# Earlier first half of a final norm, and attention heads that turn in two events, in a one-layer macaron block

## The chip, the cores and the metric

The program runs on one core of a Trainium2 chip. The core has a matrix engine (TensorE, PE in the rows, with its weight loads as PEld), a vector engine (VectorE, DVE), an activation engine (ScalarE, ACT), GpSimd (POOL) and an engine that mostly issues transfers (SyncE, SP). Each of them works through its own instructions in order and waits on semaphores for the others. The metric is the device time of one execution in microseconds. Profile times are microseconds from the first instruction of one profiled execution.

## The reference

For 512 tokens of 1024 features, everything in 32-bit floats, the program computes

```python
x = x + 0.5 * swiglu(rmsnorm(x, ffn1_norm), w_gate1, w_up1, w_down1)      # 2816 wide
x = x + token_mixer(rmsnorm(x, mix_norm), w_in, w_out, ...)
x = x + 0.5 * swiglu(rmsnorm(x, ffn2_norm), w_gate2, w_up2, w_down2)
return rmsnorm(x, final_norm)
```

The mixer has 4 differential heads (two 64-wide query/key maps and one 128-wide value each) and 8 dilated heads. A differential head is

```python
p = softmax(q @ k.T * scale + bias)          # causal, for both maps
a = p[:, :, 0] - lam * p[:, :, 1]
out = rmsnorm(a @ v, subln_gain) * (1 - lam0)
```

so a query block i of 128 tokens needs the key blocks 0 to i: 1, 2, 3 and 4 blocks of 128x128 for the four query blocks, 10 in all. `rmsnorm(x, g)` is `x * rsqrt(mean(x*x) + 1e-6) * g`.

## The kernel before

The residual x lies transposed in SBUF: eight tiles x[0..7] of 128 features by 512 tokens. Weights and activations are split in a high part of a faster number format and a low rest (fp32r in the rows), and each product is three matrix products (`mm3`, lines 123 to 125). Where an operand isn't split (turns, values, sums for a norm), the product runs in plain 32-bit floats: a value product of 128x128 is then two instructions on TensorE, a turn (a transposition against the identity) one.

**Mixer.** TensorE's stream is a list of chunks: per unit "q0, v0, q1, v1, q2, q3, q4, v2, q5, q6, v3, q7" eight chunks. A q chunk has 6 products of 512 columns, a v chunk 12 of 256 columns. `put(t, rank, f)` hangs work on chunk t: before the chunk's own products, by rank, come the events of rank under 10. TensorE, VectorE and ScalarE get exactly this order (manual schedule), so all three queues are set by the table of chunk numbers at the end of `attention`. A head u that starts at chunk s (12, 29, 45 and 53 for the differential heads 0 to 3) does:

- `score(m, i)` (TensorE L1058 and L1059, VectorE L1061, ScalarE L1064) for map m of query block i at chunk s + 2i + m. The scores lie in PSUM tiles "s", of which there are two: a score waits until VectorE has read the one before the last.
- `combine(i)` (VectorE L1068, L1071, L1075) at s + 2i + 3: it makes the weighted difference of the two maps.
- `turn(0, i)` at s + 5 + 2i: i + 1 transpositions (L1127) into a PSUM tile "t" (two of these) and a ScalarE copy to SBUF (L1130). `values(0, i)` two chunks later: i + 1 products with the values (L1139), so values(i) and turn(i+1) stand at the same chunk. Five chunks have such an event.
- from chunk e = s + 14: `squares` (ScalarE), `mean` and the root's steps (VectorE), `scale` (VectorE L1162), `finish` (four transpositions L1168 into a "t" tile, and ScalarE), `finish_low` (VectorE L1182), at e, e+1, e+2, e+3, e+4, e+6, e+7.

Dilated heads (4 to 7) have their own functions (`turn_part`, L1094 and L1105, two "t" tiles per event), with one SBUF tile "tx".

**The last stage.** The second FFN ends with products for half the tokens at a time: for feature tiles 6 and 7 first the left 256 tokens (`plb`), then the right ones (`prb`); each is 6 steps k of three products. While the right ones run, `last` lets the left half's final norm begin: sums of squares on TensorE (L1375), root and reciprocal with a correction step (`final_rstd`), a diagonal from it (L1400), a product that spreads it over all partitions (L1405), then VectorE multiplies (L1412) and SyncE writes out. After the last right product, `final_end` does the same for the right half by transpositions (L1423), scaling (L1432, L1434) and five output transfers (L1437).

Of the kernel before, what the change touches and what calls it, by code (L numbers as in the profile page):

```python
# [14 lines left out]
F32 = mybir.dt.float32  # L15
# [3 lines left out]
ALU = mybir.AluOpType  # L19
AX = mybir.AxisListType  # L20

P = 128
S = 512
D = 1024
FF = 2816
KD = D // P
JF = FF // P
HD = 64
NQ = S // P
EPS = 1e-6  # L30
# [13 lines left out]
PLAIN = 6  # L44
# [10 lines left out]
HS = S // 2  # L55
# [4 lines left out]
OFF = [0, 128, 384, 768]  # L60
# [3 lines left out]
def tile_macaron(ctx: ExitStack, tc, xs, xT, wf, wgu1, wst1, wd1, wdg1, wqk, wv, wo, wgu2, wst2, wd2,  # L64
                 wdg2, lams, relb, onehot, addc, out):
    nc = tc.nc
    V, A, G, T = nc.vector, nc.scalar, nc.gpsimd, nc.tensor
# [4 lines left out]
    tp = ctx.enter_context(tc.tile_pool(name="tp", bufs=2))  # L72
    wp = ctx.enter_context(tc.tile_pool(name="wp", bufs=3))
    sp = ctx.enter_context(tc.tile_pool(name="sp", bufs=4))
# [6 lines left out]
    def mm_bank(nm):  # L81
        return pp.tile([P, S], F32, tag="mm", name=nm, bufs=4)
# [651 lines left out]
    with tc.manual_schedule(engines={mybir.EngineType.DVE, mybir.EngineType.Activation}):  # L734
        for t in range(4):
            raw = wp.tile([P, 1024], F32, tag="raw", name=f"raw_f{t}")
            h, l = w_place()
            for kk in range(2):
                k = 2 * t + kk
# [134 lines left out]
    def put(t, rank, f, *a):  # L874
        at.setdefault(t, []).append((rank, f, a))
# [163 lines left out]
    def attention(u, s):  # L1039
# [80 lines left out]
                             skip_group_check=True)  # L1120
                n += w

        def turn(m, i):
            w = (i + 1) * P
            pt = pp.tile([P, S], F32, tag="t", name=f"pt{u}{m}{i}", bufs=2)
            for k in range(i + 1):
                T.transpose(pt[:, k * P:(k + 1) * P],  # L1127
                            st["pr"][m][:, OFF[i] + k * P:OFF[i] + (k + 1) * P], ident[:])
            ptb = tp.tile([P, S], F32, tag="ptb", name=f"ptb{u}{m}{i}", bufs=2)
            A.copy(ptb[:, :w], pt[:, :w])  # L1130
            st["ptb", m, i] = ptb

        def values(m, i):
            if "po" not in st:
                st["po"] = mm_bank(f"po{u}")
                st["po3"] = st["po"][:].rearrange("p (i d) -> p i d", i=NQ)
            fo = (u % 4) * P
            for k in range(i + 1):
                T.matmul(st["po3"][:, i, :], st["ptb", m, i][:, k * P:(k + 1) * P],  # L1139
                         vt[0, k][:, fo:fo + P], start=k == 0, stop=k == i)  # L1140

        def squares():
            ob_ = tp.tile([P, S], F32, tag="ob", name=f"ob{u}")
# [51 lines left out]
            put(s + step * i + (1 if quick else 3 if diff or i < 3 else 2),  # L1195
                5 if diff or quick or i != 2 else 6.5, combine, i)
        if diff:
            tv = max(s + 5, v_end[u])
            for i in range(NQ):
                put(tv + 2 * i, 2, turn, 0, i)  # L1200
                put(tv + 2 * i + 2, 1, values, 0, i)
            e = tv + 9
            put(e, 7, squares)
            put(e + 1, 7, mean)
            for j in range(4):
                put(e + 2 + j // 2, 8, lambda j=j: st["rs"][j]())
            put(e + 4, 7, scale)
            put(e + 6, 3, finish)
            put(e + 7, 8, finish_low)
        elif quick:  # L1210

            for j, part in enumerate((((0, 0, 3),), ((1, 1, 3), (2, 2, 3)),
                                      tuple((k, 3, 4) for k in range(NQ)))):
                for m in range(2):
                    put(s + 4 + j, 2, turn_part, m, part)
                put(s + 5 + j, 1, values_part, part)
            put(s + 7, 3, finish)
            put(s + 7, 4, finish_low)
        else:
            tv = max(s + 9, v_end[u])  # L1220
            parts = ((0, 0, 4),), ((1, 1, 4),), ((2, 2, 4), (3, 3, 4))
            for j, part in enumerate(parts):
                for m in range(2):
                    put(tv + j, 2, turn_part, m, part)
                put(tv + 4, 1, values_part, part)
            put(tv + 5, 3, finish)
            put(tv + 5, 8, finish_low)
# [110 lines left out]
    def last(t, m, o, k, put):  # L1338


        hh = int(o == "r")
        c = half(hh)
        if k == PLAIN:
            q = fin.setdefault("sq", {})
            if m not in q:
                q[m] = slot(8 + m - (KD - 2), f"sql{m}")
            put(t, A.activation, q[m][:, c], x[m][:, c], AF.Square)
            put(t, weighted, m, hh)
            if m == KD - 2 and o == "l":
                put(t, lambda: V.tensor_tensor(sq[:, c], sq[:, c], q[m][:, c], op=ALU.add))  # L1350
            if (o, m) == ("r", KD - 1):
                put(t, final_end)
        elif (o, m, k) == ("l", KD - 2, 0):
            A.activation(root[:], eps[:], AF.Sqrt)
        elif (o, m, k) == ("r", KD - 2, PLAIN - 4):
            final_sums(0, sq, True, False)
        elif (o, m, k) == ("r", KD - 2, PLAIN - 3):
            final_sums(0, fin["sq"][KD - 1], False, True)
            final_rstd(0)
            spread_parts()  # L1360
        elif (o, m, k) == ("r", KD - 1, PLAIN - 4):
            final_spread()
            final_left(0)
            final_left(1)
            final_left(2, 0, 1)

    def final_sums(hh, src, first, end):

# [9 lines left out]
    def final_rstd(hh):  # L1378
        ps, n = fin["ps", hh], NQ // 2
        y = sp.tile([P, n], F32, tag="ly", name=f"ly{hh}")  # L1380
        t = sp.tile([P, n], F32, tag="lt", name=f"lt{hh}")
        w = sp.tile([P, n], F32, tag="lw", name=f"lw{hh}")
        A.activation(y[:], ps[:, :n], AF.Sqrt, bias=eps[:])
        V.tensor_scalar(w[:], ps[:, :n], EPS, -0.5, op0=ALU.add, op1=ALU.mult)
        V.reciprocal(y[:], y[:])

        for i in range(n):
            c = slice(i, i + 1)
            V.scalar_tensor_tensor(t[:, c], y[:, c], w[:, c], y[:, c], op0=ALU.mult, op1=ALU.mult)
        V.scalar_tensor_tensor(y[:], t[:], 1.5, y[:], op0=ALU.add, op1=ALU.mult)  # L1390
        fin["y", hh] = y

# [15 lines left out]
    def final_left(g2, a=0, b=2):  # L1408
        n = b - a
        r = fin["pb"][:, :HS].rearrange("p (o q) -> p o q", o=1).to_broadcast([P, n, HS])  # L1410
        y2 = fin[0, g2][:, a * HS:b * HS].rearrange("p (m q) -> p m q", m=n)
        V.tensor_tensor(y2, y2, r, op=ALU.mult)  # L1412
        m = 2 * g2 + a
        nc.sync.dma_start(
            out[0, m * P * HS:(m + n) * P * HS].rearrange("(m p q) -> p m q", p=P, q=HS), y2)
# [23 lines left out]
            fin[b, g4, "o"][:, c0:c1])  # L1439

    def final_end():
        final_left(2, 1, 2)
        final_left(3)
        final_sums(1, sq, True, False)
        final_sums(1, fin["sq"][KD - 2], False, False)
        for m in (0, 1):
            for b in range(2):
                turned(m, b)
        final_sums(1, fin["sq"][KD - 1], False, True)
        for m in range(2, KD):  # L1450
            for b in range(2):
                turned(m, b)
        final_rstd(1)
        final_right(0, 0, V, 0, HS)
        right_out(0, 0, 0, HS)
        final_right(1, 0, A)
        final_right(0, 0, V, HS, S)
        right_out(1, 0)
        right_out(0, 0, HS, S)
        final_right(0, 1, V)  # L1460
        final_right(1, 1, A)
        right_out(0, 1)
        right_out(1, 1)
# [105 lines left out]
```

## Time and profile before

| | |
|---|---|
| three runs | 931.29, 931.54, 931.55 us; median 931.54 |
| the profiled execution | 932.39 us; from first to last instruction 930.6 us |
| TensorE busy | 922.9 us (99%), granted clock 0.999 of full |
| VectorE, ScalarE, GpSimd busy | 727.9 (78%), 543.5 (58%), 98.3 us (11%) |
| transfers | 136.71 MB, 147 GB/s mean |
| the mixer's chunks | about 345 to 552 us |
| last right-half product to the end | about 921.0 to 930.6 us |

The profiled execution took 0.85 us more than the median, of which its span is 930.6 and 1.79 lie around it. A matrix instruction's duration overlaps with the next one's, so what it costs is read from the distance of two starts. "Busy" TensorE can also hold a short wait, which then shows as a longer distance and duration, not as idle time.

### The profile page before, as it was taken

The numbers are of one execution on the slowest core, as the hardware profiler recorded it, in microseconds if no ns is written. First come the engines' busy times: TensorE is split into PE (matmuls) and PEld (weight loads), VectorE is DVE, ScalarE is ACT, GpSimd is POOL, SyncE is SP. The second block draws the span as 40 slices with busy tenths as digits, with TensorE's granted clock in tenths as the row PEclk, the third lists the DMA queues.
The fourth block names the chain that finished last, engine by engine and source line by source line (L and its number), as shares of the span: only waits on it lengthen the run. The fifth ranks groups of instructions, "written<-read, shape, count | busy, mean of one in ns | idle before, by whom it ended". The sixth has DMA issues, their size and how long they took to land.

```text
span 930.6 us, 17116 instructions
## 1 busy us (share of the span) xinstructions
PE 922.9 (99%) x6402; PEld 854.7 (92%) x6402; DVE 727.9 (78%) x1504; ACT 543.5 (58%) x1122; POOL 98.3 (11%) x117
## 2 busy tenths in 40 slices
PE   9999999999999999999999999999999999999997
PEld 8888999999999999988979778889999999999997
DVE  7797887677888897668876556797888777888784
ACT  7454665355665575656766664455666455665573
POOL 0001100112202100000000003110120012111000
PEclk9999999999999999999999999999999999999999
DMA  7446646578757562434343213464774678875542
GB/s 260 121 144 154 158 122 177 138 182 210 201 131 207 138 176 94 132 97 129 97 136 92 68 48 133 114 173 102 183 189 120 162 199 193 209 178 153 136 126 91
DMA packets 59876, 136.71 MB, mean 147 GB/s; under 512 B 6848, under 2 KB 8128, under 8 KB 59792
## 3 DMA queue, kind: packets, MB, share of 16 engines
q1 hardware_dynamic: 45792, 110.14, 36.8%
q0 software_dynamic: 14000, 25.47, 17.6%
q8 instruction: 50, 0.82, 0.4%
q14 instruction: 34, 0.28, 0.1%
HBM read 130.30 MB, written 2.14 MB: 142 GB/s over the span
## 4 chain that ended last, share of the span: by engine, by line
PE 97%; DVE 2%; DMA 0%; issue 0%; ACT 0%; DVEq 0%; SPq 0%
PE pv L935 2%; PE pv L933 2%; PE pv L934 2%; PE pq L123 2%; PE pwo L123 2%; PE pq L124 2%; PE pq L125 2%; PE pk L125 2%; PE pk L123 2%; PE pk L124 2%; PE pwo L124 2%; PE pwo L125 2%; PE pua L125 2%; PE pua L124 2%; PE pua L123 2%; PE pda L124 1%
## 5 line engine op out<-in xcount | busy, mean ns | idle before, releaser
L1064 ACT ACTIVATE pr<-pr,mx 128x128 f32<-128x128 f32 (+3 forms) x64 | 36.1, 564 | 34.3 <-DVE mx L1061 34.0
L1061 DVE CUSTOM_DVE_ANT_0 pr<-sc,strip 128x128 f32<-128x128 f32 (+3 forms) x64 | 30.7, 488 | 22.4 <-PE sc L1059 22.0
L391 ACT CAST w<-s2b 128x512 fp32r<-128x512 f32 x50 | 31.1, 621 | 17.1 <-DVE s2b L373 14.8
L395 DVE TENSOR_TENSOR w<-s2b,w 128x512 fp32r<-128x512 f32 x50 | 34.3, 686 | 7.3 <-ACT w L391 7.3
L391 ACT CAST w<-s2a 128x512 fp32r<-128x512 f32 x46 | 28.6, 622 | 17.5 <-DVE s2a L373 14.6
L395 DVE TENSOR_TENSOR w<-s2a,w 128x512 fp32r<-128x512 f32 x46 | 31.5, 686 | 6.6 <-ACT w L391 6.6
L150 POOL TENSOR_TENSOR sq<-sq,sqt 128x512 f32<-128x512 f32 x7 | 10.9, 1564 | 240.2 <-ACT sqt L149 240.1
L933 PE MATMUL pv<-w,xh 128*128 128x256 f32 x128 | 36.2, 283 | 0.0
L935 PE MATMUL pv<-w,xh 128*128 128x256 f32 x128 | 36.2, 283 | 0.0
L934 PE MATMUL pv<-w,xl 128*128 128x256 f32 x128 | 36.2, 282 | 0.0
L123 PE MATMUL pq<-xh,w 128*128 128x512 f32 x64 | 26.3, 410 | 0.0
L123 PE MATMUL pwo<-mh,w 128*128 128x512 f32 x64 | 25.5, 399 | 0.0
L124 PE MATMUL pq<-xl,w 128*128 128x512 f32 x64 | 25.1, 393 | 0.0
L125 PE MATMUL pq<-xh,w 128*128 128x512 f32 x64 | 25.0, 391 | 0.0
L125 PE MATMUL pk<-xh,w 128*128 128x512 f32 x64 | 25.0, 391 | 0.0
L123 PE MATMUL pk<-xh,w 128*128 128x512 f32 x64 | 25.0, 391 | 0.0
L124 PE MATMUL pk<-xl,w 128*128 128x512 f32 x64 | 25.0, 391 | 0.0
L124 PE MATMUL pwo<-ml,w 128*128 128x512 f32 x64 | 25.0, 390 | 0.0
L125 PE MATMUL pwo<-mh,w 128*128 128x512 f32 x64 | 24.9, 390 | 0.0
L934 PEld LDWEIGHTS pv<-w,xl 128*128 128x128 f32 x128 | 24.4, 191 | 0.3
L933 PEld LDWEIGHTS pv<-w,xh 128*128 128x128 f32 x128 | 24.4, 191 | 0.2
L935 PEld LDWEIGHTS pv<-w,xh 128*128 128x128 f32 x128 | 24.5, 191 | 0.0
(709 smaller groups left out, 3997.9 us busy)
## 6 DMA issues: line engine op xcount, KB each, us to landing
raw_qk<-wqk_dram SPq DMA_DIRECT2D x16, 512.0 KB, 3.4
raw0bg<-wst_dram SPq DMA_DIRECT2D x9, 512.0 KB, 4.8
raw_gua<-wgu_dram SPq DMA_DIRECT2D x8, 512.0 KB, 3.5
raw0ag<-wst_dram SPq DMA_DIRECT2D x8, 512.0 KB, 4.7
raw0ad<-wdg_dram SPq DMA_DIRECT2D x8, 512.0 KB, 4.7
strip<-bias_rows SPq DMA_DIRECT2D x16, 256.0 KB, 3.7
raw_v<-wv_dram SPq DMA_DIRECT2D x8, 512.0 KB, 3.3
raw_wo<-wo_dram SPq DMA_DIRECT2D x8, 512.0 KB, 3.3
```

The source lines that it names most:

```text
L123: T.matmul(po, wh, mh, start=first, stop=False, skip_group_check=on)
L124: T.matmul(po, wh, ml, start=False, stop=False, skip_group_check=on)
L125: T.matmul(po, wl, mh, start=False, stop=last, skip_group_check=on)
L150: G.tensor_tensor(sq[:], sq[:], t[:], op=ALU.add)
L391: A.copy(made[t][0], source(t))
L395: V.tensor_tensor(l, source(t), h.bitcast(F32), op=ALU.subtract)
L933: T.matmul(po, xh[k][:, xs], wh[:, o:o + 256], start=k == 0, stop=False)
L934: T.matmul(po, xl[k][:, xs], wh[:, o:o + 256], start=False, stop=False)
L935: T.matmul(po, xh[k][:, xs], wl[:, o:o + 256], start=False, stop=k == KD - 1)
L1061: V.tensor_tensor_reduce(out=pi, in0=ps[:, :w], in1=st["b"][m][:, w - 1::-1], op0=ALU.add, op1=ALU.min, scale=1.0, scalar=3.0e38, accum_ou ...
L1064: A.activation(pi, pi, AF.Exp, scale=-1.0, bias=st["mx"][:, m, i:i + 1], accum_out=st["ls"][:, m, i:i + 1])
```

## The change

Differential heads: `turn` takes tuples of query blocks, each tuple shares one PSUM tile "t" and one ScalarE copy, and the copies go to the "tx" tile. Blocks 0 and 2 (1 + 3 transpositions) share a tile, block 1 has its own, both at chunk s + 8; block 3 at s + 10. All ten value products run at s + 12 (or at the end of the v unit, if that is later), and e comes one chunk earlier.

Final norm: both sums of the left half are made at the same step (k = 2 of the right product of tile 6), the spread product and the first multiplications come after k = 1 instead of k = 2 of tile 7, the multiplication of feature tiles 4 and 5 is no longer cut in two, and `final_rstd` has other operations.

```diff
+        def turn(tiles):
+            if "tx" not in st:
+                st["tx"] = tp.tile([P, 12 * HS], F32, tag="tx", name=f"ptx{u}", bufs=1)
+            for own in tiles:
+                pt = pp.tile([P, S], F32, tag="t", name=f"pt{u}{own[0]}", bufs=2)
+                n, c0 = 0, st.get("used", 0)
+                for i in own:
+                    st["place", i] = c0 + n
+                    for k in range(i + 1):
+                        o = OFF[i] + k * P
+                        T.transpose(pt[:, n:n + P], st["pr"][0][:, o:o + P], ident[:])
+                        n += P
+                A.copy(st["tx"][:, c0:c0 + n], pt[:, :n])
+                st["used"] = c0 + n
+        def values():
...
+            for i in range(NQ):
+                for k in range(i + 1):
+                    o = st["place", i] + k * P
+                    T.matmul(st["po3"][:, i, :], st["tx"][:, o:o + P],
+                             vt[0, k][:, fo:fo + P], start=k == 0, stop=k == i)
...
         if diff:
-            tv = max(s + 5, v_end[u])
-            for i in range(NQ):
-                put(tv + 2 * i, 2, turn, 0, i)
-                put(tv + 2 * i + 2, 1, values, 0, i)
-            e = tv + 9
+            put(s + 8, 2, turn, ((0, 2), (1,)))
+            put(s + 10, 2, turn, ((3,),))
+            tv = max(s + 12, v_end[u])
+            put(tv, 1, values)
+            e = tv + 1
...
             final_sums(0, sq, True, False)
-        elif (o, m, k) == ("r", KD - 2, PLAIN - 3):
             final_sums(0, fin["sq"][KD - 1], False, True)
             final_rstd(0)
             spread_parts()
-        elif (o, m, k) == ("r", KD - 1, PLAIN - 4):
+        elif (o, m, k) == ("r", KD - 1, PLAIN - 5):
             final_spread()
             final_left(0)
             final_left(1)
-            final_left(2, 0, 1)
...
-        V.tensor_scalar(w[:], ps[:, :n], EPS, -0.5, op0=ALU.add, op1=ALU.mult)
         V.reciprocal(y[:], y[:])
-        for i in range(n):
-            c = slice(i, i + 1)
-            V.scalar_tensor_tensor(t[:, c], y[:, c], w[:, c], y[:, c], op0=ALU.mult, op1=ALU.mult)
+        V.scalar_tensor_tensor(t[:], y[:], -0.5, y[:], op0=ALU.mult, op1=ALU.mult)
+        V.scalar_tensor_tensor(t[:], ps[:, :n], EPS, t[:], op0=ALU.add, op1=ALU.mult)
...
     def final_end():
-        final_left(2, 1, 2)
+        final_left(2)
```

TensorE's queue where head 2 (chunks 51 to 53) is scored, before: `sc` is a score, `pt` a turn, `po` a value product, and the left-out rows are chunk products.

```order
L1058 MATMUL sc_5052<-k_4811,q_4809 128x512
L1059 MATMUL sc_5052<-l_4813,q_4809 128x512
...
L1139 MATMUL po_5063<-v_4247,ptb_5034 128x128
L1127 MATMUL pt_5065<-ident,pr_4864 128x128 x2
L1058 MATMUL sc_5073<-k_4812,q_4810 128x512
L1059 MATMUL sc_5073<-l_4814,q_4810 128x512
...
L1058 MATMUL sc_5087<-k_4960,q_4958 128x256
L1059 MATMUL sc_5087<-l_4962,q_4958 128x256
```

The same place in the changed kernel:

```order
L1058 MATMUL sc_5038<-k_4804,q_4802 128x512
L1059 MATMUL sc_5038<-l_4806,q_4802 128x512
...
L1058 MATMUL sc_5052<-k_4805,q_4803 128x512
L1059 MATMUL sc_5052<-l_4807,q_4803 128x512
...
L1134 MATMUL pt_5067<-ident,pr_4858 128x128 x4
L1134 MATMUL pt_5073<-ident,pr_4858 128x128 x2
L1058 MATMUL sc_5077<-k_4950,q_4948 128x256
L1059 MATMUL sc_5077<-l_4952,q_4948 128x256
```

No turn or value product stands any more between the scores of head 2; its first turn event, with the blocks 0, 2 and 1, stands right before head 3's first score, one chunk after head 2's last score.

TensorE's queue around `finish` of head 3 (`ot`, four transpositions), after the last turn event of dilated head 4 (`pt`), before and then in the changed kernel:

```order
L1094 MATMUL pt_5576<-ident,pr_5215 128x128 x3
L1094 MATMUL pt_5581<-ident,pr_5216 128x128 x3
L123 MATMUL pq_5590<-xh_78,w 128x512
...
L125 MATMUL pk_5591<-xh_78,w 128x512
L1168 MATMUL ot_5607<-ident,ob_5471 128x128 x4
```

```order
L1094 MATMUL pt_5556<-ident,pr_5204 128x128 x3
L1094 MATMUL pt_5561<-ident,pr_5205 128x128 x3
L1175 MATMUL ot_5568<-ident,ob_5438 128x128 x4
L123 MATMUL pq_5578<-xh_78,w 128x512
```

The chunk that stood between them is now behind: three tiles "t" are wanted in a row, of which there are two.

VectorE's queue at the end (the multiplications of the left half by `bcl`, and the last right product's sum into x[7], written `x_103<-prb`), before and then in the changed kernel:

```order
L1412 TENSOR_TENSOR y_10053<-y_10053,bcl 128x512
L1412 TENSOR_TENSOR y_10189<-y_10189,bcl 128x512
L1412 TENSOR_TENSOR y_10315<-y_10315,bcl 128x256
L432 SCALAR_TENSOR_TENSOR x_103<-prb_10509,x_103 128x256
L1412 TENSOR_TENSOR y_10315<-y_10315,bcl 128x256
L1412 TENSOR_TENSOR y_10442<-y_10442,bcl 128x512
```

```order
L1414 TENSOR_TENSOR y_10033<-y_10033,bcl 128x512
L1414 TENSOR_TENSOR y_10169<-y_10169,bcl 128x512
L432 SCALAR_TENSOR_TENSOR x_103<-prb_10487,x_103 128x256
L1414 TENSOR_TENSOR y_10295<-y_10295,bcl 128x512
L1414 TENSOR_TENSOR y_10422<-y_10422,bcl 128x512
```

One multiplication of 256 columns moved from ahead of the sum into x[7] to behind it, joined to its other half.

## Rows read from the trace of the kernel before

**Rows 1.** The page's line of busy times, with share of the span and instructions.

```profile
PE 922.9 (99%) x6402; PEld 854.7 (92%) x6402; DVE 727.9 (78%) x1504; ACT 543.5 (58%) x1122; POOL 98.3 (11%) x117
```

**Rows 2.** All waits of TensorE: total us, times, longest.

```profile
PE warm L725 <- POOL ones_d L719: 1.0, 1, 1.0
PE pga L770 <- ACT w L750: 0.2, 1, 0.2
```

**Rows 3.** Timeline of TensorE, an event of head 1: start, us, instruction, count.

```profile
415.01 0.83 PE L1139 MATMUL po<-v,ptb 128*128 128x128 f32 x6
415.68 0.60 PE L1127 MATMUL pt<-ident,pr 128*128 128x128 f32 x4
...
416.35 0.40 PE L124 MATMUL pq<-xl,w 128*128 128x512 f32 x1
```

**Rows 4.** Timeline of TensorE, scores of head 2 and the chunk between.

```profile
436.38 0.38 PE L1127 MATMUL pt<-ident,pr 128*128 128x128 f32 x2
436.75 0.50 PE L1058 MATMUL sc<-k,q 128*128 128x512 f32 x1
...
437.33 0.39 PE L123 MATMUL pq<-xh,w 128*128 128x512 f32 x1
...
438.70 0.32 PE L1058 MATMUL sc<-k,q 128*128 128x256 f32 x1
```

**Rows 5.** Timeline of VectorE, the same stretch.

```profile
436.14 0.55 DVE L1061 CUSTOM_DVE_ANT_0 pr<-sc,strip 128x384 f32<-128x384 f32 x1
...
436.61 0.75 DVE L1182 SCALAR_TENSOR_TENSOR ml<-ot,sub,mh 128x512 fp32r<-128x512 f32 x1
...
438.94 0.62 DVE L1075 SCALAR_TENSOR_TENSOR pr<-pr,cc,pr 128x384 f32<-128x384 f32 x1
```

**Rows 6.** Timeline of VectorE, combinations of heads 1 (two) and 3.

```profile
408.49 0.62 DVE L1075 SCALAR_TENSOR_TENSOR pr<-pr,cc,pr 128x384 f32<-128x384 f32 x1
...
412.18 0.75 DVE L1075 SCALAR_TENSOR_TENSOR pr<-pr,cc,pr 128x512 f32<-128x512 f32 x1
...
454.01 0.62 DVE L1075 SCALAR_TENSOR_TENSOR pr<-pr,cc,pr 128x384 f32<-128x384 f32 x1
```

**Rows 7.** Timeline of TensorE where chunks 37 and 61 begin (61 with a score).

```profile
410.13 0.39 PE L123 MATMUL pq<-xh,w 128*128 128x512 f32 x1
...
455.90 0.28 PE L1058 MATMUL sc<-k,q 128*128 128x256 f32 x1
```

**Rows 8.** Timeline of TensorE, the last turn event of head 4.

```profile
478.55 0.82 PE L1094 MATMUL pt<-ident,pr 128*128 128x128 f32 x6
```

**Rows 9.** Timeline of ScalarE, the copies of that event.

```profile
479.07 0.86 ACT L1105 COPY ptx<-pt 128x384 f32<-128x384 f32 x2 [1.18 <-PE pt L1094]
```

**Rows 10.** ScalarE's copies by shape: count, total us, mean ns, idle before.

```profile
L1105 ACT COPY ptx<-pt 128x384 f32<-128x384 f32 x12 | 5.2, 484 | 3.7 <-PE pt L1094 3.6
```

**Rows 11.** Timeline of TensorE, the end.

```profile
920.71 0.28 PE L125 MATMUL prb<-ahb,w 128*128 128x256 f32 x1
...
921.64 0.63 PE L1423 MATMUL ft<-ident,y 128*128 128x128 f32 x4
922.42 0.61 PE L1375 MATMUL st_n<-ones_d,sql 128*128 128x1 f32 x4
```

**Rows 12.** Timeline of VectorE, the end.

```profile
919.96 1.62 DVE L1412 TENSOR_TENSOR y<-y,bcl 128x512 f32<-128x512 f32 x3 [0.37 <-PE bcl L1405]
921.50 0.42 DVE L432 SCALAR_TENSOR_TENSOR x<-prb,x 128x256 f32<-128x256 f32 x1
...
923.36 0.16 DVE L1384 TENSOR_SCALAR lw<-st_n 128x2 f32<-128x2 f32 x1 [0.51 <-ACT ly L1383]
...
924.27 1.53 DVE L1434 TENSOR_SCALAR o<-ft,ly 128x256 f32<-128x256 f32 x3
```

**Rows 13.** Timeline of ScalarE, the end.

```profile
921.95 0.42 ACT L420 ACTIVATE sql<-x 128x256 f32<-128x256 f32 x1 [1.50 <-DVE x L432]
```

**Rows 14.** Timeline of SyncE's queue, output transfers of the right half.

```profile
924.79 2.57 SPq L1437 DMA_DIRECT2D out_dram<-o  x5
```

More of the change, by code (lines that the diff above doesn't have):

```diff
@@ L1121, in values_part @@
                 n += w
[L1123 to L1136, printed above, removed]
-            fo = (u % 4) * P
-            for k in range(i + 1):
-                T.matmul(st["po3"][:, i, :], st["ptb", m, i][:, k * P:(k + 1) * P],
-                         vt[0, k][:, fo:fo + P], start=k == 0, stop=k == i)
+        def turn(tiles):
[13 more added lines that the diff above has]
+        def values():
+            st["po"] = mm_bank(f"po{u}")
+            st["po3"] = st["po"][:].rearrange("p (i d) -> p i d", i=NQ)
+            fo = (u % 4) * P
+            for i in range(NQ):
[3 more added lines that the diff above has]
+                             vt[0, k][:, fo:fo + P], start=k == 0, stop=k == i)
         def squares():
@@ L1381, in final_rstd @@
         t = sp.tile([P, n], F32, tag="lt", name=f"lt{hh}")
-        w = sp.tile([P, n], F32, tag="lw", name=f"lw{hh}")
         A.activation(y[:], ps[:, :n], AF.Sqrt, bias=eps[:])
-        V.tensor_scalar(w[:], ps[:, :n], EPS, -0.5, op0=ALU.add, op1=ALU.mult)
         V.reciprocal(y[:], y[:])
-        for i in range(n):
-            c = slice(i, i + 1)
-            V.scalar_tensor_tensor(t[:, c], y[:, c], w[:, c], y[:, c], op0=ALU.mult, op1=ALU.mult)
+        V.scalar_tensor_tensor(t[:], y[:], -0.5, y[:], op0=ALU.mult, op1=ALU.mult)
+        V.scalar_tensor_tensor(t[:], ps[:, :n], EPS, t[:], op0=ALU.add, op1=ALU.mult)
         V.scalar_tensor_tensor(y[:], t[:], 1.5, y[:], op0=ALU.add, op1=ALU.mult)
```

## The prediction

> **What bounds the kernel now.** I read the page's busy times first, then TensorE's waits, then TensorE's timeline at every place that the change touches, with the other engines' timelines beside it. TensorE is busy for 99% of the span, VectorE for 78%, ScalarE for 58% [rows 1]. The list of TensorE's waits has two entries, 1.2 us in all, both at the start [rows 2]. So nearly all of the 930.6 us is TensorE's stream, and only three things can move the time by much: a different amount of work on TensorE, a wait inside its stream, and the stretch after its last large product, where the other engines finish alone. I take the change by these three.
>
> **The turns and values: TensorE's own work.** Before and after, a differential head has 10 turn instructions and 20 value instructions (10 products of two). What is worth asking is whether five events cost more than three, since each breaks into a stream of another number format. The event of head 1 with 6 value and 4 turn instructions answers it: from 415.01 to the second product of the stream at 416.35 are 1.34 us; the stream's own first product in it takes 0.23 (a chunk of six goes from 437.33 to 438.70, [rows 4], so 1.37 / 6); 1.11 is left for 10 instructions, 0.11 each [rows 3]. The event costs its instructions and nothing on top. The first stream product behind it does look late (0.31 to the next start instead of 0.23), but the last turn's 0.11 begins only 0.03 before it, so one pays for the other. Term 1: 0 us; bounds 0 and, if each of the 8 events that go did hide 0.03, -0.2.
>
> **Head 2: TensorE now arrives before VectorE.** What moves is 0.55 us of such work per head (turn 0, values 0 and turn 1: five instructions of 0.11) from between the scores to after them. Where TensorE arrives at a score with time to spare on VectorE's side, this costs nothing. In head 2 it doesn't: the turns that begin at 436.38 take 0.22, to 436.60, yet the next score starts at 436.75 and holds TensorE until 437.33, 0.58 where two such products take 0.46 [rows 4]. It waited 0.27 (0.15 and 0.12) for the PSUM tile that VectorE's L1061 let go at 436.14 + 0.55 = 436.69 [rows 5]. So VectorE is the late one here. If its times stay, TensorE comes to that score 0.55 earlier, starts no sooner, and the 0.55 is paid later. Then the first turn event stands at 438.70 [rows 4]; after block 0's turn (0.11, to 438.81) it needs the combination of block 2, which ends at 438.94 + 0.62 = 439.56 [rows 5]: 0.75 more. Upper bound 1.3. Against this, `scale` and `finish_low` of head 1 come one chunk earlier; the latter is 0.75 on VectorE, and it stands at 436.61 just between the reading of the scores and that combination [rows 5]. It still has to be done, earlier, where VectorE waits for the root's steps and products. If VectorE gains all of it, the combination ends at 438.8 and nothing is waited for there, and TensorE's 0.27 goes as well: lower bound -0.27. I take 0.45, near the middle, because half of the 0.75 should come through: the score's own tile is let go ahead of that instruction. What is queued behind a waiting turn is the whole of TensorE's stream; nobody but TensorE loses by it at once.
>
> **Heads 0, 1 and 3.** In head 1 the combination of block 2 ends at 408.49 + 0.62 = 409.11 [rows 6], and chunk 37 begins at 410.13 [rows 7], from which the 0.55 that moved away is taken off: TensorE arrives at 409.58, 0.47 late enough. Block 3's turn comes 0.66 (six turns) and two chunks of 1.37 later, 412.98, and its combination ends at 412.93 [rows 6]: just in time, a hop between engines aside. Head 3 arrives at 455.90 - 0.55 = 455.35 [rows 7] for a combination that ends at 454.63 [rows 6]. Head 0 looks like head 1. Term 3: 0.05; bounds 0 and 0.5, as little separates them in head 1. The large value event (20 x 0.11 = 2.2 us) hides behind nothing and needs nothing hidden: its input copies are ordered two chunks ahead, as before.
>
> **`finish` of head 3.** The six transpositions of head 4's last event end, for TensorE, at 478.55 + 6 x 0.11 = 479.21 [rows 8]. Before, a chunk stood between them and head 3's `ot`; now `ot` is next and needs a third "t" tile. The first of the two is free when ScalarE's first copy has ended: 479.07 [rows 9] + 0.48 [rows 10] = 479.55, and a hop of 0.06. TensorE waits 0.40. Should it be the second copy, it is 479.93 [rows 9], and the wait 0.78. Lower bound 0, if ScalarE came sooner. Term 4: +0.40.
>
> **The end.** The last right product starts at 920.71 and ends at about 920.99 [rows 11], but VectorE adds it into x[7] only at 921.50, because three multiplications of the left half, begun at 919.96, are ahead of it [rows 12]. Without the short one, and with the spread product one step k earlier (0.35, an estimate: three products of 256 columns at half of 0.23), the first two end near 920.9, and the sum starts at about 921.04 instead: 0.46. ScalarE's square follows (921.95 before, [rows 13]), and would end at 921.91. Then the next limit comes: TensorE's four transpositions from 921.64 leave it free only at about 922.11 [rows 11], and the last sums of squares started at 922.42: so 0.31 is won of the 0.46. The small operations from 923.36 to the scaling at 924.27 take 0.91 [rows 12]; four in a row at 0.16 and a hop of 0.04 each make 0.80, with the last hop 0.84: 0.07 more. The five output transfers go out one after the other from 924.79 [rows 14], behind the scaling, so all of it comes through to the end. Multiplying tiles 4 and 5 in one piece now falls behind the sum, where VectorE has time until 923.0. Term 5: -0.38; bounds -0.25 and -0.5.
>
> **Sum.** 0 + 0.45 + 0.05 + 0.40 - 0.38 = +0.5 us on the profiled execution's 932.39; the same on the median of the runs shown, 931.54, gives 932.1 us. The lower ends add to -1.0 (930.6), the upper ones to +2.4 (933.9).
>
> **Rivals.**
> - *VectorE's lateness goes, only the end counts.* If `scale` and `finish_low` one chunk earlier free VectorE in time and `ot` finds its tile, head 2's old wait goes: -0.27 - 0.38 = -0.65, 930.9 us. For it: 0.75 of VectorE's work leaves the tight place. Against: VectorE has to do it in the same stretch. Chance 0.20.
> - *Coarse events make TensorE wait throughout, slower.* The mechanism is one: turns now stand one chunk behind a combination, with no TensorE work between the scores to cover VectorE. With VectorE's times as they are, head 2 costs 1.3; head 3, scored right behind it, the 0.5 that I hold as upper bound; `ot` 0.78; with the end, 1.3 + 0.5 + 0.78 - 0.38 = +2.2, 933.7 us. It decides when the combination of head 2's block 2 ends later than about 439.2. For it: the 0.27 that TensorE waits there already. Against: heads 0 and 1 have 0.47. The Trainium skill, "Perfetto Trace Analysis", section "Optimizing Scalar/DVE Operations", says that where ScalarE and VectorE are not saturated but cause gaps on other engines, smaller instructions may let work end sooner; the change goes the other way with ScalarE's copies, and the 58% and 78% busy of this trace are the case it speaks of. By that rule the sum would be this rival's, not mine. Chance 0.10.
> - *Breaking into the stream does cost.* If the longer distance behind an event (0.31 against 0.23) were a price of its own, 8 events fewer would give -0.64 and all in all about -0.1 or, with the first rival, -1.3: 930.2 to 931.4 us. The 1.11 us for 10 instructions [rows 3] speaks against it. Chance 0.07.
> - *The end doesn't gain.* If the sum into x[7] isn't what the end hangs on, as when the left half's transfers hold SyncE, term 5 goes: +0.9, 932.4 us. The right half's first transfer leaves 0.03 after its data [rows 12, 14], which speaks against it. Chance 0.06.
> - *Something that no row shows* makes it faster by more than 2 us: 0.03.
>
> **How the numbers follow.** My own case has 0.54, with a range of its own from 931.6 to 932.9. A measurement of this kernel tells some 0.2%, 1.9 us, from no change: below 929.7 or above 933.4. The first, third and fourth rival and mine lie inside; the second lies mostly beyond (0.08 of its 0.10 and 0.01 of my upper tail); only the last gives faster. So faster 0.03, same 0.88, slower 0.09. The range from 930.7 to 933.3 holds all of my case and most of the first rival and leaves out, on either side, a little under one in ten.
>
> **What would show it.** Per head, turns and values of the changed kernel should still take 0.11 an instruction; a shorter or longer mean breaks term 1. In head 2, the score at chunk 52 and the third turn of the first event should start late, behind L1061 and L1075; if neither does, the first rival holds. `ot` of head 3 should start some 0.4 behind the end of the turns ahead of it. At the end, the sum into x[7] should start 0.05 behind the last product and the last sums of squares 0.3 sooner after it than now. The forecast is wrong if a wait on TensorE of over 1 us shows anywhere, or if its stream outside these places has changed.

## The result, and the profile after

The changed kernel takes **934.23 us** (median of 7 runs, 933.83 to 934.69) against 931.54 for the kernel before (7 runs, 931.20 to 931.79): a ratio of 1.0028, 95% interval 1.0018 to 1.0038. It is 2.7 us slower; the forecast was 932.1, with a range that ended at 933.3.

The page's line of busy times, answering [rows 1], and all waits of TensorE, answering [rows 2] (columns: who, for whom; us in total, times, longest):

```profile
PE 923.5 (99%) x6402; PEld 854.4 (92%) x6402; DVE 728.1 (78%) x1501; ACT 542.4 (58%) x1118; POOL 98.2 (11%) x117
```

```profile
PE warm L725 <- POOL ones_d L719: 1.0, 1, 1.0
PE pt L1094 <- DVE pr L1080: 1.0, 1, 1.0
PE pt L1134 <- DVE pr L1075: 0.7, 1, 0.7
PE sc L1058 <- DVE mx L1061: 0.5, 1, 0.5
PE ot L1175 <- ACT ptx L1105: 0.2, 1, 0.2
```

The engines do the same work, TensorE still looks 99% busy, but four waits are new, all in the mixer. The list understates them, since a short wait hides in the busy time. So I also took, for every TensorE instruction, the distance to the next start, less the plain distance of its form (0.23 us for 512 columns, 0.17 for 384, 0.12 for 256, 0.11 for 128), and summed that by stretch; such a surplus is called a loss or a wait below. All kernels, with those of the experiments further down, stand in one table: us more than the kernel before by stretch; the mixer's length from the start of its first chunk product to that of the last product with `w_out` (234.44 us before); the time from the start of the last large product to the end; and the median less that of the before runs on the same chip.

| kernel | heads 0, 1 | head 2 | head 3 | head 4's turns | `ot` of head 3 | mixer | end | median |
|---|---|---|---|---|---|---|---|---|
| before | 0 | 0 | 0 | 0 | 0 | 0 | 9.90 | 0 |
| changed | +0.01 | +0.80 | +0.94 | +1.18 | +0.43 | +3.39 | 9.16 | +2.69 |
| e1, finish later | +0.17 | +1.48 | -0.03 | -0.04 | +0.02 | +1.61 | 9.15 | +0.85 |
| e2, mean later | 0 | +0.80 | +0.18 | +1.71 | +0.41 | +3.13 | 9.19 | +2.19 |
| e3, turns back | +0.10 | +0.22 | 0 | +1.17 | +0.43 | +1.93 | 9.16 | +1.21 |
| e4, end only | -0.01 | 0 | +0.01 | -0.02 | +0.01 | -0.03 | 9.14 | -0.90 |
| e5, heads only | -0.01 | +0.80 | +0.91 | +1.20 | +0.43 | +3.35 | 9.84 | +3.46 |
| e6, before, mean earlier | 0 | +0.01 | +0.01 | +1.65 | -0.01 | +1.66 | 9.90 | +1.72 |
| e7, mean and root behind | 0 | +1.56 | -0.03 | +0.70 | +0.44 | +2.71 | 9.16 | +2.02 |
| e8, left part whole | 0 | 0 | +0.01 | -0.01 | 0 | +0.01 | 9.25 | -0.72 |
| e9, root's operations | 0 | -0.01 | +0.01 | -0.02 | +0.01 | 0 | 9.89 | -0.21 |
| e10, first turns later | +0.13 | +1.46 | -0.01 | -0.04 | +0.01 | +1.58 | 9.18 | +0.78 |
| e11, combine behind | -0.01 | +1.66 | -0.02 | -0.01 | +0.01 | +1.65 | 9.15 | +0.82 |
| e12, both turns later | +0.01 | +0.59 | 0 | -0.04 | 0 | +0.55 | 9.16 | -0.25 |
| e13, values only | +0.13 | +0.24 | +0.01 | -0.04 | 0 | +0.35 | 9.16 | -0.70 |
| e14, turn behind | -0.01 | +1.13 | 0 | -0.01 | 0 | +1.11 | 9.16 | +0.34 |

For the changed kernel the mixer's +3.39 and the end's -0.74 make +2.65, next to +2.69 by the medians; its profiled span is only 2.3 us longer, since its mixer happened to begin 0.34 earlier.

**Head 2.** TensorE where [rows 4] stood, then VectorE where [rows 5] stood:

```profile
435.51 0.39 PE L125 MATMUL pk<-xh,w 128*128 128x512 f32 x1
436.39 0.50 PE L1058 MATMUL sc<-k,q 128*128 128x512 f32 x1 [0.49 <-DVE mx L1061]
...
438.33 1.02 PE L1134 MATMUL pt<-ident,pr 128*128 128x128 f32 x6
439.11 0.36 PE L1058 MATMUL sc<-k,q 128*128 128x256 f32 x1
```

```profile
432.15 0.75 DVE L1189 SCALAR_TENSOR_TENSOR ml<-ot,sub,mh 128x512 fp32r<-128x512 f32 x1
...
435.77 0.55 DVE L1061 CUSTOM_DVE_ANT_0 pr<-sc,strip 128x384 f32<-128x384 f32 x1
...
437.92 0.62 DVE L1075 SCALAR_TENSOR_TENSOR pr<-pr,cc,pr 128x384 f32<-128x384 f32 x1
```

The score starts 0.88 after a product that takes 0.23: 0.65 of waiting behind L1061. `finish_low` of head 1 has left the tight place (432.15; it stood at 436.61, [rows 5]), so the combination ends at 438.54, and the six turns behind it hold TensorE 0.78 to the next start, where the same event of head 1 holds it 0.58. Block 3's turn, a little later, loses another 0.10.

**Head 3.** TensorE, VectorE and ScalarE of the changed kernel, then VectorE of the kernel before:

```profile
455.81 0.27 PE L1134 MATMUL pt<-ident,pr 128*128 128x128 f32 x1
456.75 0.77 PE L1134 MATMUL pt<-ident,pr 128*128 128x128 f32 x5 [0.67 <-DVE pr L1075]
```

```profile
455.23 0.22 DVE L1162 SCALAR_TENSOR_TENSOR f<-ss,kapt,cs 128x4 f32<-128x4 f32 x1 [0.82 <-ACT ob L1154]
455.49 0.23 DVE L1163 TENSOR_SCALAR ss<-ss,kape 128x4 f32<-128x4 f32 x1
455.62 0.16 DVE L1068 RECIPROCAL rl<-ls 128x2 f32<-128x2 f32 x1
...
456.08 0.62 DVE L1075 SCALAR_TENSOR_TENSOR pr<-pr,cc,pr 128x384 f32<-128x384 f32 x1
```

```profile
453.71 0.35 ACT L1154 ACTIVATE ob<-po,cs 128x128 f32<-128x128 f32 x1
...
454.74 0.37 ACT L1154 ACTIVATE ob<-po,cs 128x128 f32<-128x128 f32 x1
```

```profile
453.55 0.16 DVE L1068 RECIPROCAL rl<-ls 128x2 f32<-128x2 f32 x1
...
455.78 0.22 DVE L1155 SCALAR_TENSOR_TENSOR f<-ss,kapt,cs 128x4 f32<-128x4 f32 x1 [0.40 <-ACT ob L1147]
```

Before, head 3's combination of block 2 began at 453.55, and head 2's `mean` waited for the squares behind it. One chunk earlier, `mean` (L1162) stands ahead: VectorE idles 0.82 for ScalarE's four squares, and the combination of [rows 6] ends at 456.70 instead of 454.63. The turn waits 0.83.

**Head 4 and `ot`.** VectorE, TensorE, and ScalarE's copies that answer [rows 9]:

```profile
472.94 0.22 DVE L1162 SCALAR_TENSOR_TENSOR f<-ss,kapt,cs 128x4 f32<-128x4 f32 x1 [0.82 <-ACT ob L1154]
...
475.53 0.16 DVE L158 TENSOR_SCALAR yi_a<-ss 128x4 int32<-128x4 int32 x1
...
476.31 0.16 DVE L164 SCALAR_TENSOR_TENSOR yi_a<-yt_a,yi_a 128x4 f32<-128x4 f32 x1
476.40 0.16 DVE L1068 RECIPROCAL rl<-ls 128x2 f32<-128x2 f32 x1
476.59 0.49 DVE L1080 TENSOR_SCALAR pr<-pr,rl 128x512 f32<-128x512 f32 x1
```

```profile
475.65 0.49 PE L1094 MATMUL pt<-ident,pr 128*128 128x128 f32 x3
477.13 0.77 PE L1094 MATMUL pt<-ident,pr 128*128 128x128 f32 x5 [0.99 <-DVE pr L1080]
...
481.17 0.82 PE L1094 MATMUL pt<-ident,pr 128*128 128x128 f32 x6
482.23 0.66 PE L1175 MATMUL ot<-ident,ob 128*128 128x128 f32 x4 [0.24 <-ACT ptx L1105]
```

```profile
481.69 0.86 ACT L1105 COPY ptx<-pt 128x384 f32<-128x384 f32 x2 [1.19 <-PE pt L1094]
```

VectorE of the kernel before, with `mean` (L1155), the same combination (from L1068 on) and the first root step:

```profile
473.19 0.22 DVE L1155 SCALAR_TENSOR_TENSOR f<-ss,kapt,cs 128x4 f32<-128x4 f32 x1
...
473.59 0.16 DVE L1068 RECIPROCAL rl<-ls 128x2 f32<-128x2 f32 x1
...
474.19 0.16 DVE L158 TENSOR_SCALAR yi_a<-ss 128x4 int32<-128x4 int32 x1
```

The same for the dilated head 4, which the diff does not touch: `mean` of head 3 and five small root instructions (475.53 to 476.40) stand ahead of its last combination. The third turn's successor starts 1.26 after it instead of 0.11, so TensorE waits 1.15. Before, that combination began at 473.59, `mean` found its squares done, and the root steps came after. `ot` waits 0.40 behind the six turns of [rows 8], for the first copy.

**The end.** VectorE, TensorE's last sums of squares and SyncE, answering [rows 12], [rows 11] and [rows 14]; the last large product starts at 923.76:

```profile
924.08 0.42 DVE L432 SCALAR_TENSOR_TENSOR x<-prb,x 128x256 f32<-128x256 f32 x1
924.42 1.27 DVE L1414 TENSOR_TENSOR y<-y,bcl 128x512 f32<-128x512 f32 x2
...
926.92 1.53 DVE L1436 TENSOR_SCALAR o<-ft,ly 128x256 f32<-128x256 f32 x3
```

```profile
925.16 0.51 PE L1380 MATMUL st_n<-ones_d,sql 128*128 128x1 f32 x4
```

```profile
927.43 2.32 SPq L1439 DMA_DIRECT2D out_dram<-o  x5
```

Counted from the start of the last large product, the sum into x[7] starts at 0.32 (0.79 before), the last sums of squares at 1.40 (1.71) and the scaling at 3.16 (3.56). The five transfers take 2.32 to issue (2.57).

### The profile page after: what moved, and what is told of

It is laid out like the page before. It is cut to its first block, busy times and chain, and to the rows that moved or that the text cites. A ratio compares the mean times of both kernels' runs of the same rounds, so it can differ in the third digit from the quotient of the medians.

```text
span 932.9 us, 17106 instructions
## 1 busy us (share of the span) xinstructions
PE 923.5 (99%) x6402; PEld 854.4 (92%) x6402; DVE 728.1 (78%) x1501; ACT 542.4 (58%) x1118; POOL 98.2 (11%) x117
## 4 chain that ended last, share of the span: by engine, by line
PE 94%; DVE 3%; ACT 1%; issue 1%; DVEq 0%; POOL 0%; POOLq 0%
PE pwo L123 2%; PE pwo L124 2%; PE pwo L125 2%; PE pua L123 2%; PE pua L124 2%; PE pua L125 2%; PE pv L935 1%; PE pv L934 1%; PE pv L933 1%; PE pq L123 1%; PE pq L124 1%; PE pq L125 1%; PE pk L123 1%; PE pk L125 1%; PE pk L124 1%; PE pda L125 1%
## 5 line engine op out<-in xcount | busy, mean ns | idle before, releaser
L1061 DVE CUSTOM_DVE_ANT_0 pr<-sc,strip 128x128 f32<-128x128 f32 (+3 forms) x64 | 30.7, 487 | 26.5 <-PE sc L1059 26.4
```

The costliest lines, as they stand in the source:

```text
L1061: V.tensor_tensor_reduce(out=pi, in0=ps[:, :w], in1=st["b"][m][:, w - 1::-1], op0=ALU.add, op1=ALU.min, scale=1.0, scalar=3.0e38, accum_ou ...
```

## The experiments

Theory Q: a finish one chunk earlier puts instructions that wait for ScalarE ahead of the next head's combination in VectorE's queue. Theory C, the rival of the prediction: turns in coarse events stand too close behind their combinations.

**e1_finish_later.**

```diff
-            e = tv + 1
+            e = tv + 2
```

> The changed kernel with squares, mean, root steps, scale, finish and finish_low of the differential heads one chunk later (e = s + 14, as in the kernel before); turns and values stay coarse. Theory Q (VectorE's queue: `mean` of a head now stands ahead of the next head's combination and makes VectorE wait 0.82 us for ScalarE's squares): the waits at head 3's third turn (0.83), at head 4's turn (1.15) and at `ot` of head 3 (0.40) go, 2.4 us; the stretch 431 to 446 keeps its +0.8. With the end's gain of 0.7 that is 931.5 to 931.9 us. Theory C (coarse turns stand too close behind their combinations): the turn waits stay, only `ot` may go: 933.8 to 934.2 us.

932.60 us, ratio 1.0012 (1.0003 to 1.0021). The waits at head 3's and head 4's turns and at `ot` are all gone, as Q said; C kept those at the turns. But head 2 costs 1.48, more than Q allowed, so the time is 0.7 above what I expected: `finish_low` of head 1 is back in the tight place, and the turns wait for the combination behind it. Heads 0 and 1 lose 0.17, nearly all of it at head 1's turn of block 3, which the prediction had found just in time.

```profile
436.52 0.74 DVE L1189 SCALAR_TENSOR_TENSOR ml<-ot,sub,mh 128x512 fp32r<-128x512 f32 x1
...
438.85 0.62 DVE L1075 SCALAR_TENSOR_TENSOR pr<-pr,cc,pr 128x384 f32<-128x384 f32 x1
```

```profile
438.61 0.27 PE L1134 MATMUL pt<-ident,pr 128*128 128x128 f32 x1
439.52 0.77 PE L1134 MATMUL pt<-ident,pr 128*128 128x128 f32 x5 [0.65 <-DVE pr L1075]
```

**e2_mean_later.**

```diff
-            put(e + 1, 7, mean)
+            put(e + 2, 7, mean)
```

> The changed kernel with `mean` alone one chunk later (chunk e + 2 instead of e + 1), everything else of the finish where the change put it. Theory Q: only that one move gives back the waits of head 3's turn (0.83) and head 4's turn (1.15); `ot` of head 3 keeps its 0.40 or so, as finish stays early: 932.0 to 932.5 us. Theory C: no difference to the changed kernel, 934.2 us.

933.94 us, 1.0021 (1.0013 to 1.0030). By its time alone this lies nearer to C's 934.2 than to the range for Q, but C asked for no difference, and head 3's turn got back 0.76 of 0.94, while head 4's wait grew. Q in its narrow form, `mean` alone, fell: the root steps still stand ahead of head 4's combination, now with `mean` right in front of them (474.42 to 475.82).

```profile
474.42 0.22 DVE L1162 SCALAR_TENSOR_TENSOR f<-ss,kapt,cs 128x4 f32<-128x4 f32 x1
...
475.74 0.16 DVE L164 SCALAR_TENSOR_TENSOR yi_a<-yt_a,yi_a 128x4 f32<-128x4 f32 x1
475.82 0.16 DVE L1068 RECIPROCAL rl<-ls 128x2 f32<-128x2 f32 x1
```

**e3_turns_back.**

```diff
-            put(s + 8, 2, turn, ((0, 2), (1,)))
-            put(s + 10, 2, turn, ((3,),))
+            for i in range(NQ):
+                put(s + 5 + 2 * i, 2, turn, ((i,),))
```

> The changed kernel with the turns at the chunks of before (block i at s + 5 + 2i, a tile and a copy each), all values still in one event at s + 12 and the finish still one chunk early. Theory Q: head 4's wait (1.15) and `ot`'s (0.40) stay, as no turn of head 4 was moved; head 2's and head 3's waits at turns go, since a turn is again a chunk further from its combination: 932.2 to 932.7 us. Theory C: all waits at turns go, head 4's too: 930.8 to 931.4 us.

932.96 us, 1.0013 (1.0004 to 1.0022), 0.26 above the range for Q. Head 4's 1.17 and `ot`'s 0.43 stayed although the turns were fine again: C does not explain them. Head 3's wait went, since its turn stands a chunk further away and hides the late combination.

**e4_end_only** (the diff of the final norm alone, on the kernel before).

> The kernel before with the change of the end alone (both sums of the left half at one step, spread and multiplications one step earlier, multiplication of tiles 4 and 5 whole, other operations in final_rstd). Both theories: the output transfers of the right half leave 0.4 us earlier; if the further 0.33 us by which the changed kernel's last transfers were shorter is real, 0.7: 930.8 to 931.2 us. If the end gains nothing, 931.5 us.

930.85 us, 0.9992 (0.9983 to 1.0001): the mixer is that of before, and the end takes 9.14 us instead of 9.90. It is the lowest median of all; its interval just reaches 1.

**e5_heads_only** (the diff of the heads alone).

> The changed kernel without the change of the end: differential heads only. If the two parts add, the mixer's +3.4 us in full and the end at 9.90 us after the last large product: 934.8 to 935.3 us. If a part of the mixer's loss is taken up further on, less.

935.34 us, 1.0042 (1.0028 to 1.0055). The two parts add.

**e6_mean_earlier**, on the kernel before:

```diff
-            put(e + 1, 7, mean)
+            put(e, 7.5, mean)
```

> The kernel before, with one thing changed: `mean` of the differential heads stands at chunk e (right behind `squares`) instead of e + 1, so that VectorE meets it ahead of the next heads' combinations, as in the changed kernel. Turns and values stay fine. Theory Q (a finish instruction that waits for ScalarE, ahead of a combination in VectorE's queue): VectorE idles until the squares are done, head 4's first turns get their last combination about 1.2 us late: 932.5 to 933.2 us, and a wait on TensorE of 0.9 to 1.4 us at a turn of head 4; head 3's turns stand two chunks behind their combination and hide it. Theory C (coarse turns): nothing, 931.5 to 931.8 us.

933.54 us, 1.0018 (1.0009 to 1.0027). Only `mean`, two small VectorE instructions a head, moved in the kernel before; no turn was touched, and head 4 loses 1.65 (0.25 more than I expected). VectorE idles 2.13 for the squares:

```profile
472.37 0.22 DVE L1155 SCALAR_TENSOR_TENSOR f<-ss,kapt,cs 128x4 f32<-128x4 f32 x1 [2.13 <-ACT ob L1147]
```

```profile
PE pt L1094 <- DVE pr L1080: 1.2, 2, 0.7
```

**e7_root_behind.**

```diff
-            put(e + 1, 7, mean)
+            put(e + 2, 7, mean)
-                put(e + 2 + j // 2, 8, lambda j=j: st["rs"][j]())
+                put(e + 3 + j // 2, 8 if j < 2 else 6.9, lambda j=j: st["rs"][j]())
```

> The changed kernel with `mean` and the four root steps behind the combinations that they stood ahead of (mean at e + 2, root steps at e + 3 and e + 4, ahead of scale); squares, scale, finish and finish_low where the change put them. Moving `mean` alone gave head 3's turn its time back but not head 4's, whose combination then stood behind 0.45 us of mean and 0.95 of root steps. Theory Q in this wider form: head 4's wait goes too, while head 2's +0.8 and 0.36 at `ot` stay: 932.0 to 932.5 us. If it is the turns' own lateness: 933.9 us as with mean alone.

933.84 us, 1.0021 (1.0013 to 1.0030): missed. Head 4 keeps 0.70, by the trace for a reason on ScalarE that no run tested by itself: the squares, one chunk earlier, stand ahead of a weight cast (L893), and VectorE waits for that cast at L897, ahead of the combinations. And head 2 rises to +1.56, since head 1's steps now come later in front of its scores. Both ways of placing the early finish's steps met a combination or a score that needed VectorE.

```profile
473.06 0.69 DVE L897 TENSOR_TENSOR w<-raw_qk,w 128x512 fp32r<-128x512 f32 x1 [1.33 <-ACT w L893]
```

**e8_left_whole and e9_rstd_only**, on the kernel before: e8 has one multiplication and one transfer less ahead of `final_end`, e9 only the new operations of `final_rstd`.

```diff
-            final_left(2, 0, 1)
...
-        final_left(2, 1, 2)
+        final_left(2)
```

```diff
-        V.tensor_scalar(w[:], ps[:, :n], EPS, -0.5, op0=ALU.add, op1=ALU.mult)
...
+        V.scalar_tensor_tensor(t[:], y[:], -0.5, y[:], op0=ALU.mult, op1=ALU.mult)
+        V.scalar_tensor_tensor(t[:], ps[:, :n], EPS, t[:], op0=ALU.add, op1=ALU.mult)
```

> The kernel before with one thing of the end changed: the left half's multiplication of tiles 4 and 5 in one piece in final_end (9 output transfers instead of 10), spread product and the rest of the end as before. If the 0.35 us by which the last transfers of all kernels with the new end go out sooner come from one transfer fewer: the fifth transfer of the right half leaves 0.1 behind the fourth (0.42 before), and the time from the last large product to the end falls from 9.90 to 9.2 to 9.5 us; 930.9 to 931.3 us. If not, only the 0.2 to 0.3 of the earlier sum into x[7]: 9.6 to 9.7.

> The kernel before with the new operations of final_rstd alone. By the rows 0.07 us shorter between the sums' root and the scaling of the right half; nothing else moves: from the last large product to the end 9.83 us if the tenth transfer still waits, 931.4 to 931.7 us.

e8: 931.10 us, 0.9989 (0.9980 to 0.9998); 9.25 us after the last product. e9: 931.61 us, 0.9995 (0.9986 to 1.0004); 9.89. So of the end's 0.74, 0.65 is the short multiplication that left, with the transfer that it took along, and the new operations give nothing. Of the 0.65, 0.34 comes ahead of the scaling and the rest behind it. The right half's five transfers of e8 and e9:

```profile
923.93 2.32 SPq L1436 DMA_DIRECT2D out_dram<-o  x5
```

```profile
924.00 2.58 SPq L1434 DMA_DIRECT2D out_dram<-o  x5
```

**e10_turns_later**, on e1:

```diff
-            put(s + 8, 2, turn, ((0, 2), (1,)))
+            put(s + 9, 2, turn, ((0, 2), (1,)))
```

> The changed kernel with the finish one chunk later (as in the run that took the waits of heads 3 and 4 and of `ot` away) and, new, the first turn event of each differential head at s + 9 instead of s + 8. Theory F (fill): head 2's waits have two sources, a turn too close behind its combination (0.81 there) and a score that TensorE reaches too early because no turn or value product stands ahead of it (0.73, 0.27 in the kernel before). A later turn takes only the first away: 0.8 us less than with the turns at s + 8, about 931.6 to 931.9 us, and the score's wait still 0.6 to 0.8. Rival, VectorE behind throughout: the 0.81 reappears at the next score or turn, 932.4 to 932.7 us.

932.66 us, 1.0010 (1.0002 to 1.0019): the rival was right. The first event waits no more; TensorE reaches block 3's turn so much earlier, and waits there:

```profile
436.52 0.50 PE L1058 MATMUL sc<-k,q 128*128 128x512 f32 x1 [0.56 <-DVE mx L1061]
...
443.28 0.63 PE L1134 MATMUL pt<-ident,pr 128*128 128x128 f32 x4 [0.72 <-DVE pr L1075]
```

**e11_combine_behind**, on e4:

```diff
-                5 if diff or quick or i != 2 else 6.5, combine, i)
+                6.5 if (u, i) == (2, 1) else 5 if diff or quick or i != 2 else 6.5, combine, i)
-                put(tv + 2 * i, 2, turn, 0, i)
+                put(tv + 2 * i + ((u, i) == (2, 1)), 2, turn, 0, i)
```

> The kernel before with the change of the end, and in head 2 alone the combination of block 1 behind VectorE's reading of score (1, 2) instead of ahead of it, its turn one chunk later. The old wait of 0.27 at the score of chunk 52 goes if that combination (0.9 us) is what makes VectorE late there: mixer 0.2 to 0.3 us shorter than with the end alone (234.41 us from its first to its last product of the plan), 930.5 to 930.8 us. If something else makes it late, no difference: 930.9.

932.70 us, 1.0010 (1.0002 to 1.0019). The score waits no more, so the combination was what made it late; but the turn's copy now stands behind another activation and a weight cast in ScalarE's queue, and a value product waits 1.5 us for it (1.3 in the list of waits).

```profile
PE po L1139 <- ACT ptb L1130: 1.3, 1, 1.3
```

**e12_both_later**, on e10, which left head 2 open:

```diff
-            put(s + 10, 2, turn, ((3,),))
+            put(s + 11, 2, turn, ((3,),))
```

> The changed kernel with finish one chunk later (e = s + 14) and both turn events one chunk later (blocks 0, 2 and 1 at s + 9, block 3 at s + 11, where blocks 2 and 3 turned in the kernel before). Theory D (distance: a turn needs two chunks behind its combination): no wait at any turn is left; what stays is the 0.72 at the score of chunk 52 (0.27 before), as nothing stands ahead of it: mixer 234.8 to 235.0 us, 931.2 to 931.6 us. Rival, VectorE behind in head 2 whatever stands where: a wait of 0.8 shows at some turn or value again, 932.4 to 932.8 us.

931.61 us, 0.9997 (0.9988 to 1.0006). Theory D holds: two coarse events with the distance that blocks 2 and 3 had before, and no wait at a turn is left. The one wait is the score's:

```profile
PE warm L725 <- POOL ones_d L719: 1.0, 1, 1.0
PE sc L1058 <- DVE mx L1061: 0.6, 1, 0.6
PE pga L770 <- ACT w L750: 0.2, 1, 0.2
```

**e13_values_only**: e1 and e3 together.

> The changed kernel with turns at the chunks of before (each block its own tile and copy) and the finish at its old place; of the change in the heads only the values in one event is left. If turns and finish are the whole loss: mixer 234.4 to 234.7 us, 930.8 to 931.3 us. If the values in one event cost by themselves (nothing between the scores of head 2 but turns): 0.2 us more at head 2, as in the run with turns alone put back.

931.16 us, 0.9994 (0.9985 to 1.0003). The values in one event cost 0.35 by themselves: 0.24 at head 2, as between its scores there are only turns now, and 0.13 in small pieces ahead of it, which no wait names.

**e14_turn_behind**: e11, with the turn of block 1 behind the score in its old chunk.

```diff
+                put(tv + 2 * i, 6.5 if (u, i) == (2, 1) else 2, turn, 0, i)
```

> The kernel before with the change of the end, and in head 2 alone the combination of block 1 behind VectorE's reading of score (1, 2), and its turn behind score (1, 3) in the same chunk. A try at a version better than both: where the turn went a chunk later, the score's wait was gone but a value product waited 1.5 us for its copy. With the turn in its chunk the copy comes in time: mixer 234.1 to 234.3 us, 930.5 to 930.7 us. If the copy is late again: 931.5 us or more.

932.20 us, 1.0005 (0.9996 to 1.0014). The copy is late again, if less. The old 0.27 is cheaper than either cure.

```profile
440.45 0.71 PE L1139 MATMUL po<-v,ptb 128*128 128x128 f32 x4 [0.82 <-ACT ptb L1130]
```

## Why the prediction was wrong, point by point

- **Term 1, TensorE's own work, 0.** Right: heads 0 and 1 differ by 0.01 over 86 us. Fewer, larger events save nothing.
- **Term 2, head 2, +0.45 (-0.27 to 1.3).** +0.80: the mechanism was right, the size too low. The score at chunk 52 costs 0.49 of the 0.55 in the upper bound, the late combination about 0.3 of the 0.75. What I argued against each other showed apart: with the whole finish back at its old place it is +1.48 (e1), above the upper bound of 1.3, so the earlier finish gives 0.68, close to the 0.75 of `finish_low`; and where no turn waits any more, 0.59 stays, for want of the products that stood between the scores (e12).
- **Term 3, heads 0, 1 and 3, +0.05 (0 to 0.5).** This step failed. It compared TensorE's arrival with the end of head 3's combination at 454.63 as the trace of before shows it. But that time was no longer given: the finish of head 2 had moved one chunk earlier, past that very combination. Measured +0.94, of which 0.76 is `mean` alone (e2).
- **A term that is missing: head 4, +1.18.** The same step, left out for the next head. I used the earlier finish only where it helps (head 2) and at `ot`, and never walked `squares`, `mean` and the root steps past what they overtake on VectorE and ScalarE. e6 shows the mechanism in the kernel before, by moving `mean` alone, and e1 takes both losses away. The sign of being wrong that the prediction named, a wait of over 1 us, stands here (1.15). These two places are 2.1 us, the size of the whole miss (934.2 against 932.1); head 2's further 0.35 and the end's further 0.36 cancel. The upper bounds add to 2.33 (the prediction's 2.4 is a slip), so the measured 2.69 lies beyond them all.
- **Term 4, `ot`, +0.40.** Right: the wait is 0.40, for the first copy, and the stretch costs 0.43.
- **Term 5, the end, -0.38 (-0.25 to -0.5).** Direction right; -0.74 measured. The scaling did come 0.40 sooner, near the 0.38, but that is luck: the last sums of squares start 0.31 sooner, as the term had it, and also take 0.10 less (0.51, [rows 11] has 0.61), while `final_rstd` gives nothing (e9) instead of 0.07, as a gap of 0.11 opens between its second and third operation. The term put nothing behind the scaling, and 0.33 was won there: 0.25 in the issue of the last five transfers, 0.08 after it. Of ten output transfers the last left 0.42 after the issue of the ninth had ended; of nine, the last left 0.10 after. No row of before that I used separated this.
- **The rivals.** The one on the slower side, coarse events, gave 933.7 and 0.10. It named head 2, head 3 and `ot`, and the price is near, yet only part of it is its mechanism: the turns' nearness is worth 0.9 at head 2 (e1 against e12), at head 3 it costs only where the finish is early too (e1 and e3 each have 0 there), and head 4 has nothing to do with it (e3). The Trainium skill, "Perfetto Trace Analysis", section "Optimizing Scalar/DVE Operations", was cited there for smaller instructions that end sooner. No run here bears that out as the cause: with the same three coarse copies two chunks behind the combinations (e12), no turn waits; against e1, which differs from it in the turns' chunks alone, moving them was enough. No run made the copies smaller at the same chunk, so what size alone does is not shown. The rival by which only the end counts has its figure, 930.9, at e4 (930.85), but by chance: there head 2's old wait of 0.27 is still there, and the end gives twice its 0.38. The rival by which breaking into the stream costs falls with term 1, and the one by which the end gains nothing with e4's 9.14 against 9.90.

What stays open: why SyncE holds back the tenth transfer. The end alone (e4) has the lowest median of all, 0.9 below the kernel before, but its interval just reaches 1, and e8 and e13 are too near to be told from it.

## What to carry to other kernels

When an edit moves a chain of small instructions one slot earlier, list for every engine what the chain now overtakes, and treat each overtaken instruction's time in the old trace as void; a helper of the next unit that the diff does not touch can be the one that loses. An instruction that waits for another engine is dearest just ahead of a result that the bottleneck needs. Work that seems to interrupt the busy engine may be what covers the other engines between two waits: taken out and batched, it saves nothing and uncovers them.

## What the runs showed of the hardware

SyncE's last transfer: with ten output transfers at the end (before, e5, e6, e9) the five of the right half take 2.57 to 2.58 us to issue, with nine (all others) 2.32 to 2.33, in every profile. And a TensorE that the page calls 99% busy before and after lost 3.4 us more in the mixer of the changed kernel, of which the list of waits names 2.4, while its busy time rose by 0.6.
